# Loads held back where the attention's zone opens, and a second bank for retention's products

## The chip, the cores and the metric

The kernel runs on one core of a Trainium2 chip. The core has a matrix engine (PE, with a queue of weight loads PEld), VectorE (DVE), ScalarE (ACT), GpSimd (POOL) and a queue (SP) from which all of this kernel's transfers between the chip's memory and the core are issued. The engines run side by side and wait for each other through semaphores. The metric is the time of one execution in device microseconds (us), the median of several runs.

## The reference

One layer of a streaming encoder works on a prompt of 2048 rows and on a sample of 64 rows whose stream already has 4096 past rows. Rows are normalised and multiplied with one wide input weight; its columns feed a differential attention (four heads, queries and keys in two halves of 64, values of 128), a retention (four heads of 128, computed in chunks with a state that is carried on), a gate for each, and two merging gates. Both branches are projected, merged, projected once more and added to the input.

```python
h = rmsnorm(x, norm_g) @ w_in
qa, ka, va, za, qb, kb, vb, zb, ga, gb = jnp.split(h, _split_points(), axis=-1)
# attention: a = softmax(q0 k0) - lam * softmax(q1 k1), chunk-causal, with a distance bias
s = jnp.einsum('bqhcd,bkhcd->bhcqk', q, k) * (DK_A ** -0.5)
a = p[:, :, 0] - lam * p[:, :, 1]
# retention: inside a chunk, and across chunks by a state r
s = jnp.einsum('bnthd,bnshd->bnhts', qc, kc) * d_intra
intra = jnp.einsum('bnhts,bnshe->bnthe', s, vc)
return decay_c * r + u_n, r
cross = jnp.einsum('bnthd,bnhde,ht->bnthe', qc, r_before, xi)
...
m = ga * (oa @ w_oa) + gb * (ob @ w_ob)
return x + m @ w_out
```

Keys, values and the retention state are outputs too.

## The kernel before, in words

All products run at full precision by splitting a float32 operand into a high and a low part (names hi and lo, `thi` and `tlo`, `wh` and `wl`): three products stand for one. ACT copies the high part, DVE or POOL subtracts it for the low part.

The work has three zones. In the first the prompt's first half and the sample are projected (`w_stream`, line 2594 and after; its products are L997 and L847), and the sample's attention runs. In the second, the attention's zone, the second half is projected while the prompt's attention and the retention run among these products. In the third both branches are gated, projected and merged (L2302 to L2304, L2426 to L2428).

The order of PE, ACT and DVE is written out by a planner: the class keeps generators as tasks, each with a priority, and a clock in ns for each engine (`self.pe`, `self.act`, `self.dve`). `loop` (L160) always advances the task of best priority that is ready at PE's planned time; a generator that yields a time sleeps until PE's clock has reached it, one that yields a function sleeps until it is true. `take` and `give` hand out buffers and banks with the planned time at which they come free; `either` (L650) takes from whichever of several has one earliest. The projections have the last priority, so they fill PE when nothing else is ready. The order of SP and POOL isn't written out: the framework's scheduler places their instructions, and each of these queues runs in its order, so a transfer that waits holds up all behind it.

What matters here:

- `attn_zone` (L2672) opens the second zone. Then `z_stream` (L2685) starts three tasks: retention (`ret_stream`, L2071), the loading of heads (`h_loader`, L1468) and of query tiles (`q_loader`, L1455). `load_head` (L1415) takes two K buffers and two V buffers for each half of the keys; there are four of each, so in the first half of the prompt a second head can be loaded while the first is worked on. Four K transfers of 256 KB and two V transfers of 512 KB make up a head there; a query tile is four transfers of 128 KB, and two of them and the distance table `dfar` are loaded within the first head's loading.
- `qk_block` (L1498) makes score products (L1514, L1515) into a bank `s` or `tp`; DVE adds the distance table and takes the extremes (L1523); ACT exponentiates (L1554); `at_pv` (L1586) transposes (L1626) and multiplies with V (L1604 to L1606) into the bank `pv`.
- `fin_va` (L1232) ends a projected value tile: ACT copies the high part into the one `thi` buffer (L1245) and the raw values (L1247), DVE makes the low part (L1249), and three stores send them out (`vN<-thi`, `out_v_prompt`, `vN<-tlo`). The next tile's `thi` can't be written until the store of the last has landed. `fin_qk` uses the same `thi` buffer for keys and queries (L1216, L1211; stores `kT<-thi`, `qT<-thi`).
- `ret_block` (L1949) works on 128 rows of retention: it loads qbT, kbT and vbN, makes scores (L1970) in bank `s`, transposes keys in bank `at`, makes the output (L2004, L2007) in bank `pv`, normalises it, transposes it in bank `tp` (L2043) and stores it. `ret_some` runs eight blocks after loading two tables (rmask, rxi), two of them alive at a time. `ret_stream` runs blocks 0 to 7 once the first keys, queries and values are projected, and later the sample's block and blocks 8 to 15.

PSUM has eight banks: two `mm`, two `s`, two `at`, one `pv`, one `tp`.

Of the kernel before, what the change touches and what calls it, by code (L numbers as in the profile page):

```python
# [43 lines left out]
LAND = 2000.0  # L44
DMA_LAT = 2600.0
QUANT = 6
GRAIN = 64
EARLY = 7104
LATER = 12032
# [39 lines left out]
class Arena:  # L89
    def __init__(self, tile, n):  # L90
        self.tile = tile
        self.at = [0.0] * (n // GRAIN)
        self.turn = 0
# [10 lines left out]
    def place(self, sizes, now):  # L104
        got = []
        for n in sizes:
            k = -(-n // GRAIN)
            best = None
# [13 lines left out]
        t = max(max(w) for a, k, w in got)  # L122
        return [Span(self.tile[:, a * GRAIN:a * GRAIN + n], a, n) for (a, k, w), n in zip(got, sizes)], t

    def drop(self, span, t, lo, hi):
        a, b = span.start + lo // GRAIN, span.start + -(-hi // GRAIN)
        self.at[a:b] = [t] * (b - a)
        self.turn += 1
# [7 lines left out]
class Hybrid:  # L136
# [62 lines left out]
    def fits(self, n):  # L199
        w = -(-n // GRAIN)  # L200
        run = 0
        for t in self.ar.at:
            run = run + 1 if t is not None and t <= self.pe else 0
            if run == w:
                return True
        return False
# [1261 lines left out]
    def h_loader(self, half):  # L1468
        for h in range(4):
            yield from self.head_in(half, h)  # L1470
            yield from self.load_head(half, h)

    def chunks(self, nk):
        n = nk // 128
        if n <= 4:
            return [(0, nk)]
        if n > 8:
            m = [(0, 512), (512, 512)]
            return m + [(1024 + a, b) for a, b in self.chunks(nk - 1024)]
        last = 4 if n != 5 else 3  # L1480
        return [(0, nk - 128 * last), (nk - 128 * last, 128 * last)]
# [467 lines left out]
    def ret_block(self, k, t0, r, first):  # L1949
# [11 lines left out]
        t = self.ld(vb, self.vbN[t0:t0 + r, :], 1 << 18)  # L1961
# [7 lines left out]
        for h in range(4):  # L1969
            nc.tensor.matmul(s3[:, h, :], kt[:, h, :], qt[:, h, :], start=True, stop=True)  # L1970
            t = self.P(512)
        yield from self.take("at")
        kn = self.psum("at")[:r]
        for h in range(4):
            nc.tensor.transpose(kn[:, 128 * h:128 * h + 128], kt[:, h, :], self.ident)
            t2 = self.P(256)
# [19 lines left out]
            tu = self.P(512)  # L1996
        yield lambda: self.ret_at == k
        yield max(ts, self.t_state)
        yield from self.take("pv")
        state = self.state  # L2000
        op = self.psum("pv")[:r]
        for h in range(4):
            oh = op[:, 128 * h:128 * h + 128]
            nc.tensor.matmul(oh, sm[:, h, :], vb[:, 128 * h:128 * h + 128], start=True, stop=first)  # L2004
# [5 lines left out]
        if first:  # L2010
            nc.vector.tensor_copy(state, up)
            t = self.V(512, tu)
        else:
            for h in range(4):
# [3 lines left out]
                t = self.V(128, max(tu, to))  # L2018
# [7 lines left out]
        t1 = self.A(512, to)  # L2026
        nc.scalar.copy(o, op)
        t2 = self.A(512, to)
        self.give("pv", t2)
        yield t1  # L2030
        nc.vector.tensor_reduce(ms, sq.rearrange("p (h e) -> p h e", h=4), axis=AX.X, op=ALU.add)
        nc.vector.tensor_scalar(ms, ms, 1.0 / 128, EPS, op0=ALU.mult, op1=ALU.add)
# [1 line left out]
        t = self.V(80)  # L2034
# [2 lines left out]
        nc.vector.tensor_mul(o3, o3, rs.unsqueeze(2).to_broadcast([r, 4, 128]))  # L2037
        t = self.V(632, t2) + SLACK
        yield t
        yield from self.take("tp")  # L2040
        tp = self.psum("tp")[:, :4 * r]
        for h in range(4):
            nc.tensor.transpose(tp[:, r * h:r * h + r], o[:, 128 * h:128 * h + 128], self.ident[:r, :r])  # L2043
            t = self.P(256)
        res = qk[:, 0:4 * r]
        nc.scalar.copy(res, tp)
        t = self.A(4 * r, t)
        self.give("tp", t)
        yield t
        for h in range(4):  # L2050
            rh = res[:, r * h:r * h + r]
            d3 = self.obT[h].rearrange("p (g c) -> p g c", c=GW)
            if r == 128:
                g0, c0 = t0 // 256, t0 % 256
                t = self.st(d3[:, g0, c0:c0 + 128], rh, 1 << 16)
            else:
                t = self.st(d3[:, :, 256:GW], rh.rearrange("p (g c) -> p g c", c=8), 1 << 17)
# [12 lines left out]

    def ret_stream(self):  # L2071
        yield lambda: "kqv00" in self.done
        yield from self.ret_some(0, 8)
        yield lambda: "ret1" in self.done
        yield self.marks["ret1"] + 6000
        yield from self.ret_sample()
        yield from self.ret_some(8, 8)
        yield self.t_state
        self.st(self.o["ret_prompt"][0, 0].rearrange("h d e -> d h e"),
                self.state.rearrange("p (h e) -> p h e", h=4), 1 << 18)  # L2080
# [745 lines left out]
```

## Time and profile before

| | |
|---|---|
| median of three runs | 1929.72 us (1927.65 to 1930.25) |
| the profiled execution's own time | 1932.02 us |
| its span, first to last instruction | 1929.9 us |
| PE busy | 1887.0 us, 98% |
| DVE, ACT, POOL busy | 1291.6, 947.8, 587.9 us |
| granted clock of PE, mean | 0.993 |
| moved by DMA | 313.10 MB, 162 GB/s |

How to read it: PE is the busiest engine; a busy share of 98% is modelled from when products start and is no measure of their efficiency. What can be gained without changing the work is PE's idle time (1929.9 - 1887.0 = 42.9 us) and time at a lower clock. In the rows below `out<-in` names the tiles, L a line of the kernel before, `<-` in a row of waits the instruction that ended the wait.

### The profile page before, as it was taken

To read this page: it belongs to the slowest core of one execution; us is meant where nothing else is said; L and a number is where in the kernel's file an instruction comes from. 1 tells how busy PE (TensorE), PEld (TensorE's weight loads), DVE (VectorE), ACT (ScalarE), POOL (GpSimd) and SP (SyncE) were. 2 spreads that over 40 slices of the span, in tenths; PEclk is the share of its full clock that TensorE was granted. 3 is DMA by queue.
4 is the path that set the end of the run, shared out by engine and by line. 5 is a ranking of instruction groups with operands and counts; after the bars stand their busy time and mean duration, and the time that the engine had idled before them with its cause. 6 is when DMAs were issued, how large, how long until landed. Compare 5 with 4: busy or idle time off the path is not lost.

```text
span 1929.9 us, 33596 instructions
## 1 busy us (share of the span) xinstructions
PE 1887.0 (98%) x11690; PEld 1689.4 (88%) x11690; DVE 1291.6 (67%) x3058; ACT 947.8 (49%) x2151; POOL 587.9 (30%) x557
## 2 busy tenths in 40 slices
PE   9999999999995899999999999999999999999999
PEld 7788888888885899989999989999999999999887
DVE  6766766656573688775667675338877359987664
ACT  6444554444431566555456555346556455553221
POOL 2320365656540121121111111121211255522442
PEclk9999999999998899999999999999999999999999
DMA  7655455565658476455434444553441388886542
GB/s 253 215 167 138 160 170 178 177 181 177 181 162 222 146 194 194 148 162 143 131 91 134 135 115 113 141 142 92 112 121 52 113 233 272 249 264 197 185 153 77
DMA packets 361324, 313.10 MB, mean 162 GB/s; under 512 B 67906, under 2 KB 319938, under 8 KB 361155
## 3 DMA queue, kind: packets, MB, share of 16 engines
q1 hardware_dynamic: 361154, 310.97, 54.9%
q8 instruction: 92, 1.51, 0.3%
q14 instruction: 78, 0.63, 0.1%
HBM read 205.43 MB, written 104.60 MB: 161 GB/s over the span
## 4 chain that ended last, share of the span: by engine, by line
PE 89%; DVE 3%; DMA 3%; SPq 1%; issue 1%; ACT 1%; POOL 0%; DVEq 0%; ACTq 0%; POOLq 0%
PE mm L997 35%; PE mm L847 9%; PE tp L847 4%; PE at L1626 3%; PE s L1514 2%; PE s L1515 2%; PE s L847 2%; PE pv L1606 2%; PE pv L1605 2%; PE pv L1604 2%; PE s L2426 1%; PE s L2428 1%; PE s L2427 1%; SPq L234 1%; PE pv L1891 1%
## 5 line engine op out<-in xcount | busy, mean ns | idle before, releaser
L961 POOL TENSOR_TENSOR wl<-ws,wh 128x512 fp32r<-128x512 f32 x125 | 169.8, 1374 | 325.4 <-ACT wh L951 218.3
L997 PE MATMUL mm<-xh,wh 128*128 128x512 f32 (+2 forms) x768 | 257.7, 336 | 0.0
L997 PE MATMUL mm<-xh,wl 128*128 128x512 f32 (+2 forms) x768 | 251.5, 327 | 0.0
L997 PE MATMUL mm<-xl,wh 128*128 128x512 f32 (+2 forms) x768 | 251.4, 327 | 0.0
L997 PE MATMUL mm<-wh,xh 128*128 128x256 f32 (+1 forms) x760 | 248.0, 326 | 0.0
L997 PE MATMUL mm<-wh,xl 128*128 128x256 f32 (+1 forms) x760 | 242.4, 319 | 0.0
L997 PE MATMUL mm<-wl,xh 128*128 128x256 f32 (+1 forms) x760 | 242.2, 319 | 0.0
L1641 DVE TENSOR_TENSOR atl<-at,ath 128x512 fp32r<-128x512 f32 (+1 forms) x144 | 93.6, 659 | 100.1 <-ACT ath L1639 100.0
L1554 ACT ACTIVATE row<-row,a_mx 128x896 f32<-128x896 f32 (+5 forms) x144 | 149.5, 1041 | 21.3 <-DVE a_mx L1533 21.2
L997 PEld LDWEIGHTS mm<-wh,xh 128*128 128x128 f32 x760 | 144.7, 190 | 11.1 <-DVE raw L1169 0.2
L997 PEld LDWEIGHTS mm<-wl,xh 128*128 128x128 f32 x760 | 144.8, 191 | 10.8
L997 PEld LDWEIGHTS mm<-xh,wl 128*128 128x128 f32 x768 | 144.8, 189 | 10.6
L997 PEld LDWEIGHTS mm<-xh,wh 128*128 128x128 f32 x768 | 145.0, 189 | 10.4
L997 PEld LDWEIGHTS mm<-xl,wh 128*128 128x128 f32 x768 | 145.2, 189 | 10.0
L997 PEld LDWEIGHTS mm<-wh,xl 128*128 128x128 f32 x760 | 144.5, 190 | 10.6
L1639 ACT CAST ath<-at 128x512 fp32r<-128x512 f32 (+1 forms) x144 | 79.7, 564 | 146.1 <-PE at L1626 143.4
L1398 POOL TENSOR_TENSOR r_y<-r_y,r_sq 128x256 f32<-128x256 f32 x32 | 28.4, 888 | 388.4 <-DVE r_sq L1395 242.8
L1514 PE MATMUL s<-K,q 128*128 128x512 f32 (+3 forms) x242 | 91.7, 380 | 26.4 <-DVE a_acc L1523 25.7
L1523 DVE CUSTOM_DVE_ANT_0 row<-s,dfar 128x512 f32<-128x512 f32 (+2 forms) x144 | 88.9, 629 | 41.9 <-PE s L1515 41.8
L726 POOL TENSOR_TENSOR wl<-ws,wh 128x256 fp32r<-128x256 f32 x64 | 57.1, 892 | 195.8 <-ACT wh L717 190.8
L1576 DVE SCALAR_TENSOR_TENSOR row<-row,a_w 128x896 f32<-128x896 f32 (+6 forms) x88 | 98.3, 1125 | 0.0
L951 ACT CAST wh<-ws 128x512 fp32r<-128x512 f32 x128 | 76.9, 618 | 26.2 <-DMA ws<-in_w_in_dram 11.9
(488 smaller groups left out, 5464.8 us busy)
## 6 DMA issues: line engine op xcount, KB each, us to landing
ws<-in_w_in_dram SPq DMA_DIRECT2D x160, 256.0 KB, 3.3
q<-qT SPq DMA_DIRECT2D x128, 128.0 KB, 3.1
K<-kT SPq DMA_DIRECT2D x48, 256.0 KB, 4.3
V<-vN SPq DMA_DIRECT2D x24, 512.0 KB, 5.7
row<-in_x_prompt_dram SPq DMA_DIRECT2D x16, 512.0 KB, 4.7
wz<-in_w_in_dram SPq DMA_DIRECT2D x32, 256.0 KB, 4.1
row<-in_cache_k_T_dram SPq DMA_DIRECT2D x32, 256.0 KB, 3.7
row<-in_cache_v_diff_dram SPq DMA_DIRECT2D x32, 256.0 KB, 3.2
```

What stands on the lines that cost most here:

```text
L726: nc.gpsimd.tensor_sub(l[:, cs], src, h[:, cs].bitcast(F32))
L847: nc.tensor.matmul(ps, w[:, c], xs[x][c], start=bool(tag) and c == 0 and i == 0, stop=c == 3 and i == 2, skip_group_check=True)
L951: self.nc.scalar.copy(h, st)
L961: self.nc.gpsimd.tensor_sub(l, st, h.bitcast(F32))
L997: nc.tensor.matmul(ps, p, q, start=c == 0 and i == 0, stop=c == KC - 1 and i == 2)
L1514: nc.tensor.matmul(ps, q1s, kk, start=True, stop=False)
L1523: nc.vector.tensor_tensor_reduce(out=row[:, k0:k0 + n], in0=ps, in1=tab, scale=-SLOPES[h], scalar=3.0e38, op0=ALU.add, op1=ALU.min, accum_ ...
L1554: nc.scalar.activation(u, u, AF.Exp, bias=mx, scale=-1.0, accum_out=lp[:, k:k + 1])
L1576: nc.vector.scalar_tensor_tensor(out=u0, in0=u1, scalar=w[:, 0:1], in1=u0, op0=ALU.mult, op1=ALU.add)
L1626: nc.tensor.transpose(at[:, w:w + 128], src, self.ident)
L1639: nc.scalar.copy(ah[:, :w], at[:, :w])
L1641: nc.vector.tensor_sub(al[:, :w], at[:, :w], ah[:, :w].bitcast(F32))
```

## The change

Three things are edited. First, in `h_loader` the task sleeps for 18 us of PE's planned time after the first head of the first half has been loaded, before it loads the second. Second, `ret_stream` sleeps for 36 us of planned time before it loads the tables and starts its blocks. Third, the output products of a retention block, which took bank `pv`, and its transposes, which took bank `tp`, now each take whichever of the two is free earlier. The numbers of lines below the edits move by one to four in the changed kernel.

```diff
@@ constants
 QUANT = 6
+CALM = 18000.0
 GRAIN = 64
@@ h_loader
         for h in range(4):
             yield from self.head_in(half, h)
             yield from self.load_head(half, h)
+            if half == h == 0:
+                yield self.pe + CALM
@@ ret_block
         yield lambda: self.ret_at == k
         yield max(ts, self.t_state)
-        yield from self.take("pv")
+        bank = yield from self.either(1, "pv", "tp")
         state = self.state
-        op = self.psum("pv")[:r]
+        op = self.psum(bank)[:r]
...
         nc.scalar.copy(o, op)
         t2 = self.A(512, to)
-        self.give("pv", t2)
+        self.give(bank, t2)
...
-        yield from self.take("tp")
-        tp = self.psum("tp")[:, :4 * r]
+        bank = yield from self.either(1, "tp", "pv")
+        tp = self.psum(bank)[:, :4 * r]
...
         t = self.A(4 * r, t)
-        self.give("tp", t)
+        self.give(bank, t)
@@ ret_stream
         yield lambda: "kqv00" in self.done
+        yield self.pe + 2 * CALM
         yield from self.ret_some(0, 8)
```

## The prediction, made before the changed kernel ran

> **What bounds the kernel now.** I read the page first, then the waits of the matrix engine (PE) over the whole span, then the waits and the queue of the window in which the longest of them falls.
>
> The page's busy line, and of its forty slices (48.2 us each) the rows of PE and of the clock granted to it:
>
> ```profile
> PE 1887.0 (98%) x11690; PEld 1689.4 (88%) x11690; DVE 1291.6 (67%) x3058; ACT 947.8 (49%) x2151; POOL 587.9 (30%) x557
> PE   9999999999995899999999999999999999999999
> PEclk9999999999998899999999999999999999999999
> ```
>
> PE is busy nearly everywhere, so this kernel gets faster only where PE idles or runs at a lower clock. It idles 1929.9 - 1887.0 = 42.9 us, and one pair of slices (579 to 675 us) stands out, in the clock too. The waits of PE over the span, longest first (us in total, times, longest):
>
> ```profile
> PE s L1514 <- DVE a_acc L1523: 25.7, 1, 25.7
> PE at L2303 <- DVE ogl L2259: 3.8, 3, 1.8
> ```
>
> One single wait is 60% of all idle time. It lies at the opening of the attention's zone; of the waits in the window 596 to 633 us these two stand behind it:
>
> ```profile
> DVE tlo L1249 <- ACT raw L1247: 35.9, 2, 33.7
> ACT thi L1245 <- DMA vN<-thi: 33.3, 1, 33.3
> ```
>
> So PE's score product waits for a bank that VectorE (DVE) must read; DVE stands in its order behind the low half of a projected value tile; that waits for ScalarE (ACT), and ACT waits to overwrite the one thi buffer until the store of its last contents has landed. The DMA queue (SP) shows why that store is late (start us, us to issue):
>
> ```profile
> 594.91 0.34 SPq L234 DMA_DIRECT2D dnear<-in_c_dnear_dram  x1
> 595.30 2.40 SPq L234 DMA_DIRECT2D K<-kT  x4
> 597.75 5.68 SPq L234 DMA_DIRECT2D q<-qT  x8
> 603.48 0.59 SPq L234 DMA_DIRECT2D dfar<-in_c_dfar_dram  x1
> 604.11 1.06 SPq L234 DMA_DIRECT2D V<-vN  x2
> 605.21 6.05 SPq L234 DMA_DIRECT2D K<-kT  x4
> 611.31 1.91 SPq L234 DMA_DIRECT2D V<-vN  x2
> 613.27 6.54 SPq L234 DMA_DIRECT2D row<-in_c_rmask_dram  x1
> ...
> 623.38 1.58 SPq L234 DMA_DIRECT2D row<-vbN  x1
> 625.06 0.38 SPq L239 DMA_DIRECT2D vN<-thi  x1
> ```
>
> The store leaves at 625.06 behind 30 loads. The last 14 of them are head 1's K and V (heads counted from 0), from 605.21, and retention's tables and first two blocks, to 625.06: 19.9 us of the queue. The chain that ended last runs through it (start us, us):
>
> ```profile
> 611.94 11.42 DMA V<-vN
> ...
> 625.06 5.17 DMA vN<-thi
> ...
> 632.39 0.58 PE s L1514
> ```
>
> The store lands at 630.23, and 2.16 us later PE runs again.
>
> **Part 1: the 14 loads are held back (h_loader, ret_stream).** The planner's two new waits put head 1's loads 18 us, retention's 36 us of planned PE time later. In the built program the queue is the same up to the second V load; then come at once the three stores of the waiting tile, then one K load, the next tile's stores and the q loads. The number of instructions is the same on all engines (PE 11390, DVE 3060, ACT 1924, POOL 562, SP 1415 as built), so only waits can change. PE's order too is the same for its first 2,614 rows, beyond the stall, so the stall's place stays.
>
> The store can issue from 605.2. When does it land? Landings of the thi stores and of head 0's two V loads, in their windows:
>
> ```profile
> L239 SPq DMA_DIRECT2D vN<-thi x3: 360/368/379, 590.9 to 630.9; - x3
> DMA to landing us min/median/max: 2.2/2.5/5.2
> L234 SPq DMA_DIRECT2D V<-vN x2: 432/506/581, 604.1 to 604.6; - x2
> DMA to landing us min/median/max: 6.2/8.8/11.4
> ```
>
> What the 16 DMA engines moved from 594 to 606 us, and from 605 to 627:
>
> ```profile
> DMA packets 1698, 2.45 MB, mean 204 GB/s; under 512 B 208, under 2 KB 1313, under 8 KB 1698
> DMA packets 7487, 5.88 MB, mean 267 GB/s; under 512 B 293, under 2 KB 6643, under 8 KB 7486
> ```
>
> - Early end: the store does not feel the loads ahead and lands in 2.2 us, at 607.4; PE resumes at 609.6; gain 632.4 - 609.6 = 22.8 us.
> - Late end: it lands behind the second V load, which landed at 604.59 + 11.4 = 616.0; its 0.26 MB at 267 GB/s take 1.0 us; landed 617.0, PE at 619.1; gain 13.3 us.
> - My value: up to that V load 3.9 MB were issued (dnear 256, four K of 256, eight q of 128, dfar 480, two V of 512 KB). At most 2.45 MB had moved by 606; the other 1.45 MB at 267 GB/s last to 611.4, the store's own data to 612.4, and the 2.5 us of a lone store less its 1.0 us of data are 1.5 us to the landing: 613.9, PE at 616.1. I take this, nearer the late end, because that V load landed late with head 1's K loads beside it. Gain **16.3 us**.
>
> The clock. Windows around the stall (from:to, length, then busy time and count of PE, PEld, DVE, ACT, POOL; granted clock; DMA share; GB/s):
>
> ```profile
> 609.00:610.00 1.00, 0.00 (x0) 0.00 (x0) 0.00 (x0) 0.00 (x0) 0.00 (x0) 1.00 1.27 301
> 610.00:611.00 1.00, 0.00 (x0) 0.00 (x0) 0.00 (x0) 0.00 (x0) 0.00 (x0) 0.58 1.15 284
> 632.00:637.00 5.00, 4.61 (x16) 4.32 (x17) 3.32 (x17) 3.62 (x13) 2.55 (x2) 0.50 0.77 236
> 637.00:638.00 1.00, 1.00 (x8) 0.90 (x7) 0.71 (x3) 0.70 (x3) 0.83 (x1) 0.76 0.88 257
> ```
>
> PE stopped at 632.39 - 25.72 = 606.7 and the clock halved at about 610.2, 3.5 us later; after the restart it stayed at half for about 5 us, which costs 2.5 us. A stall of 616.1 - 606.7 = 9.4 us still halves it: no gain here, cost unchanged. Only at the early end (2.9 us idle) do 2.5 us come on top.
>
> The Trainium skill (TensorE: Matmul & The Clock Gate, Part 1) has the clock halve after an idle window of about 3.4 us that runs freely, and full again after about 3.4 us of work. The 3.5 us agree, the 5 us are longer here. By its figure the restart would cost some 1.7 us instead of 2.5, before and after alike, so an estimate by that page leaves the sum as it is.
>
> **What the held loads cost where they go.** Built order: three K and two V loads follow the fourth tile's stores, head 1's q loads follow, then eight retention loads, then a K load of head 2 that needs PE's last score product of head 0, and behind that the store of the first key tile's thi. PE's rate here:
>
> ```profile
> 640.00:890.00 250.00, 244.81 (x1979) 239.38 (x1978) 197.79 (x580) 146.11 (x360) 45.55 (x39) 1.00 0.58 167
> ```
>
> That is 7.9 products a us. Head 1's first score product is PE row 2858, some 240 rows past the stall's end, 30 us: even with the slowest landing quoted, 11.4 us, its K are in time if the queue reaches them within 18 us. The key store waits for row 2839, 52 rows (6.6 us) after its transposes; with 2.5 to 5.2 us to land, the buffer is free 9.1 to 11.8 us after them, and ACT wants it after row 2861, 74 rows or 9.4 us. So 0 to 2.4 us; I take **1 us** lost, inside these ends.
>
> **Part 2: retention's products and transposes take bank pv or tp.** Nothing is added. With the delay it moves the first half's blocks 2 to 7, which ran behind head 3 (PE rows 4587 to 4941), among heads 1 to 3 (all eight products in rows 3068 to 4234). Attention's last PE row goes from 7871 to 7503 while the last projection stays (8151, 8149): filler is used later, in all the same work. DVE instructions of a block:
>
> ```profile
> L1979 DVE TENSOR_TENSOR row<-s,row x17: 417/691/693, 654.8 to 1255.8; 128x512 f32<-128x512 f32 x16, 64x256 f32<-64x256 f32 x1
> L2016 DVE SCALAR_TENSOR_TENSOR row<-row,at x64: 273/284/290, 680.6 to 1263.0; 128x128 f32<-128x128 f32 x64
> L2031 DVE TENSOR_REDUCE ms<-row x17: 671/685/686, 671.5 to 1263.6; 128x4 f32<-128x512 f32 x16, 64x4 f32<-64x512 f32 x1
> L2037 DVE TENSOR_TENSOR row<-row,sm_y x17: 683/691/694, 682.8 to 1267.3; 128x512 f32<-128x512 f32 x16, 64x512 f32<-64x512 f32 x1
> ```
>
> 0.69 + 4 x 0.28 + 0.69 + 0.69 = 3.2 us a block, 19 us for six, into a window in which DVE has 250 - 198 = 52 us free. I take 0: PE's filler covers it while DVE has room. If that cover goes, all 19 us at worst; the other way, the window's own idle of 5.2 us could go, a gain of 5.2. In the last part the earlier end of attention lets output weights be split sooner; of PE's waits there (3.8 us on L2259) I count none as gone, 0 to 3.8.
>
> **Sum.** -16.3 + 1 + 0 = -15.3 us. The profiled execution took 1932.0 us (span 1929.9 and 2.1 around it), 2.3 above the median 1929.7; I carry the difference to the median: **1914.4, say 1915 us**.
>
> **Rivals.**
> - The store lands unhindered (early end): -22.8 - 2.5 + 1 = -24.3, 1905 us. For it speaks the 2.2 us; against it, that in this window transfers landed in the order of issue (V at 6.2, then 11.4 us). The Trainium skill (DMA: Bandwidth & Descriptors, on queues, rings and completion order) says that each DMA engine takes its descriptors in the ring's order; by that rule this rival falls and the sum stays at 16. No run here has yet shown a store with few loads ahead.
> - Slower: the held loads block the queue where they now stand, ahead of the key tiles' stores. Price: the same 19.9 us of queue, whole, and a second halving of the clock of 2.5: -16.3 + 19.9 + 2.5 = +6.1, 1936 us. It decides once the hold is beyond 14 us. For it: ACT again has one thi buffer, and 14 loads and a PE-bound K load stand ahead. Against: they go in two bunches and the window's DMA share is 0.58.
> - DVE becomes the bound among heads 1 to 3: half of the 19 us shows in PE: -15.3 + 9.6 = -5.7, 1924 us. For it: 0.79 of DVE busy there becomes 0.87. Against: PE lost only 5.2 us at 0.79.
> - The hold-back does not shorten the wait, because something else was late too (dnear, q or K): 1930 us. Against: of the loads ahead, the eight q were the last that the scores need, and they landed by 602.9 + 5.6 = 608.5:
>
> ```profile
> L234 SPq DMA_DIRECT2D q<-qT x8: 573/605/606, 597.7 to 602.9; - x8
> DMA to landing us min/median/max: 4.4/5.3/5.6
> ```
>
> **How the numbers follow.** Forecast 0.54, unhindered store 0.11, DVE bound 0.16, queue blocked 0.13, no effect 0.06. A measurement here tells 0.2%, 3.9 us, from no change. Faster: 0.54 + 0.11 + most of 0.16 = 0.78; same: 0.06 and the edge of the DVE case, 0.09; slower 0.13. The likeliest case alone spans 1911 to 1920 (13.3 with 2.4 lost, to 16.3 with 2.4 of the last part's 3.8 gained). The range reaches to the unhindered store and the lost effect, 1905 to 1930, and leaves out the blocked queue and the tail of the DVE case.
>
> **What would show it.** The wait of PE on L1523 near 606 us falls from 25.7 to 8 to 12 us (3 if the store is unhindered), ACT's on vN<-thi from 33.3 to about 17; the clock still halves once. SP issues vN<-thi right behind two V loads near 605 to 608. The first retention product comes after 670 us. The prediction is wrong if a new wait of ACT on kT<-thi or of PE over 10 us appears between 620 and 950 us, or if PE's idle time there passes 10 us.

## The result and the profile after

The changed kernel takes 1904.2 us (median of four runs, 1903.6 to 1906.9), the kernel before on the same chip 1929.2: a ratio of 0.9874 with a 95% interval of 0.9857 to 0.9891. It is faster by 25 us where 15 were forecast, and 0.8 us below the low end of the range. The profiled execution took 1906.88 us with a span of 1904.8, 25.1 less than the span before, so the two traces can be set against each other as they stand.

The page's busy line of the changed kernel, and of its forty slices the rows of PE and of its granted clock:

```profile
PE 1886.2 (99%) x11690; PEld 1691.2 (89%) x11690; DVE 1277.7 (67%) x3058; ACT 947.4 (50%) x2151; POOL 590.5 (31%) x557
PE   9999999999998999999999999999999999999999
PEclk9999999999998999999999999999999999999999
```

PE's busy time is the same within 0.8 us; its idle time went from 42.9 to 18.6 us. Its waits over the whole span, longest first (us in total, times, longest), and then the waits of the window 596 to 633 us:

```profile
PE s L1517 <- DVE a_acc L1526: 8.1, 2, 7.9
PE at L2307 <- DVE ogl L2263: 3.1, 3, 2.0
```

```profile
DVE tlo L1250 <- ACT raw L1248: 18.8, 3, 15.8
ACT thi L1246 <- DMA vN<-thi: 15.4, 1, 15.4
PE s L1517 <- DVE a_acc L1526: 7.9, 1, 7.9
```

The stall is at its old place with its old chain, and shorter: 7.9 us for 25.7, behind a wait of ACT on the store of 15.4 us for 33.3. The DMA queue (SP; start us, us to issue) shows the store right behind head 0's V loads, as the built order had it; the only held load that follows closely is one K load:

```profile
597.53 6.02 SPq L235 DMA_DIRECT2D q<-qT  x8
603.60 0.60 SPq L235 DMA_DIRECT2D dfar<-in_c_dfar_dram  x1
604.24 1.06 SPq L235 DMA_DIRECT2D V<-vN  x2
605.39 2.43 SPq L240 DMA_DIRECT2D vN<-thi  x1
...
608.99 0.71 SPq L235 DMA_DIRECT2D K<-kT  x1
612.87 0.35 SPq L240 DMA_DIRECT2D vN<-thi  x1
```

Those V loads, and the copy of ACT that waited for the store (the bracket is ACT's idle time and what ended it):

```profile
L235 SPq DMA_DIRECT2D V<-vN x2: 432/506/581, 604.2 to 604.7; - x2
DMA to landing us min/median/max: 5.6/6.2/6.7
```

```profile
612.26 0.59 ACT L1246 CAST thi<-mm 128x512 fp32r<-128x512 f32 x1 [15.41 <-DMA vN<-thi]
```

The slower V load took 6.7 us instead of 11.4, so it had landed by 604.7 + 6.7 = 611.4, and ACT could write thi at 612.26, where the prediction had the store landing at 613.9. A store issued at 605.39 took until 612.26, 6.9 us, though stores elsewhere land in 2.2.

The rest of the gain lies elsewhere. Windows of the changed kernel (from:to, length, then busy time and count of PE, PEld, DVE, ACT, POOL; granted clock; DMA share; GB/s), and after them the second one in the kernel before:

```profile
640.00:890.00 250.00, 249.55 (x2050) 245.68 (x2050) 197.26 (x581) 150.48 (x378) 50.27 (x42) 1.00 0.63 180
1510.00:1700.00 190.00, 186.95 (x1445) 183.43 (x1444) 134.46 (x267) 89.81 (x195) 74.84 (x65) 0.99 0.72 213
```

```profile
1510.00:1700.00 190.00, 185.53 (x1415) 180.59 (x1414) 140.25 (x256) 104.11 (x219) 95.91 (x79) 1.00 0.78 233
```

In 640 to 890 us PE idled 250 - 244.81 = 5.2 us before and idles 0.45 now; around the opening of the last zone it idled 4.5 and idles 3.05. Retention moved into the first of these windows, as one of its DVE instructions, run once per block, shows before and after (busy us, mean ns, idle us before):

```profile
L2031 DVE TENSOR_REDUCE ms<-row 128x4 f32<-128x512 f32 x2 | 1.4, 677 | 0.0
```

```profile
L2034 DVE TENSOR_REDUCE ms<-row 128x4 f32<-128x512 f32 x8 | 5.4, 678 | 0.0
```

So the 25.1 us of span are: the stall 17.8, the window behind it 4.8, the opening of the last zone 1.4, and 1.1 in small pieces (PE's busy time 0.8 of it). Of the signs that the prediction named, PE's wait came just under its 8 to 12 us, ACT's was 15.4 for about 17, retention's first output product came at 687.7 us, after 670, and no wait of ACT on kT<-thi appeared from 620 to 950 us. The clock halved once at the stall, and in this profile a second time at 1578 us.

### The profile page after: what moved, and what is told of

Read it like the earlier page. It is cut to its first block, busy times and chain, and to the rows that moved or that the text cites. A ratio compares the mean times of both kernels' runs of the same rounds, so it can differ in the third digit from the quotient of the medians.

```text
span 1904.8 us, 33589 instructions
## 1 busy us (share of the span) xinstructions
PE 1886.2 (99%) x11690; PEld 1691.2 (89%) x11690; DVE 1277.7 (67%) x3058; ACT 947.4 (50%) x2151; POOL 590.5 (31%) x557
## 5 line engine op out<-in xcount | busy, mean ns | idle before, releaser
L998 PEld LDWEIGHTS mm<-wl,xh 128*128 128x128 f32 x760 | 144.5, 190 | 10.9
L1526 DVE CUSTOM_DVE_ANT_0 row<-s,dfar 128x512 f32<-128x512 f32 (+2 forms) x147 | 90.5, 631 | 26.0 <-PE s L1518 25.4
L1307 ACT COPY ev<-mm 128x512 f32<-128x512 f32 (+2 forms) x84 | 38.6, 460 | 113.2 <-PE mm L998 105.1
```

The costliest lines, as they stand in the source:

```text
L998: nc.tensor.matmul(ps, p, q, start=c == 0 and i == 0, stop=c == KC - 1 and i == 2)
L1526: nc.vector.tensor_tensor_reduce(out=row[:, k0:k0 + n], in0=ps, in1=tab, scale=-SLOPES[h], scalar=3.0e38, op0=ALU.add, op1=ALU.min, accum_ ...
```

## The experiments

My theory was that the change is the shorter stall and nothing else: the held loads make it, the bank choice is worth 0, and all else is hidden. The rivals: that the bank choice brings part of the gain (or takes part back), that one hold alone does it, and that something besides the loads ahead of the store sets when it lands. Head 1's hold-back alone wasn't tried, nor the products' choice of bank without a hold.

A table first, worked out from the profiles: PE's idle time in us in the stall, in 640 to 890 us and in 1510 to 1700 us (length of the window less PE's busy time), the start of retention's first output product, and by how many us the attention's last V product lies ahead of the last projection product.

| kernel | median us | stall | 640-890 | 1510-1700 | retention from | attention ahead |
|---|---|---|---|---|---|---|
| before | 1929.2 / 1927.3 | 25.7 | 5.2 | 4.5 | 667 | 49 |
| after | 1904.2 | 7.9 | 0.45 | 3.05 | 688 | 110 |
| holds without bank choice | 1923.8 | 8.4 | 0.06 | 13.2 | 901 | 33 |
| transposes' bank choice alone | 1925.2 | 22.8 | 3.45 | 2.7 | 664 | 62 |
| retention's hold alone | 1915.8 | 16.8 | 2.35 | 0.5 | 685 | 83 |
| retention's hold, bank choice | 1912.2 | 17.1 | 1.2 | 0.5 | 681 | 109 |
| after, first V loads later | 1900.4 | 6.3 | 0.0 | 0.7 | 686 | 110 |
| both holds, retention's short, no choice | 1906.5 | 8.1 | 4.1 | 1.0 | 657 | 59 |
| after, hold of 19 us | 1903.2 | 8.0 | 1.05 | 1.1 | 687 | 110 |
| before with a second thi buffer | 1912.1 | 15.7 | 0.13 | 2.0 | 657 | 53 |

(1929.2 is the kernel before beside the first run of the changed kernel, 1927.3 beside the others but the last two of this section.)

**Both holds, the bank choice undone.**

```diff
-        bank = yield from self.either(1, "pv", "tp")
+        yield from self.take("pv")
...
-        bank = yield from self.either(1, "tp", "pv")
+        yield from self.take("tp")
```

> Both hold-backs, without the choice of bank (pv and tp as before). The opening of the zone is the changed kernel's, so the wait of PE near 606 us is 7.9 us by every theory. Theory 'bank' (the choice of bank gives the 6 us gained outside that wait): PE idles some 5 us in 640 to 890 us as before, and the time is about 1910 us. Theory 'hold' (the loads and retention standing later gives them): PE idles under 1 us there, 1904 us. Theory 'order' (any new order of the planner falls somewhere within some us): either, without rule.

Measured: 1923.84 us, ratio 0.9982 (0.9972 to 0.9991). None of the theories had this time: the window from 640 to 890 us idles 0.06 us, the sign of 'hold', but 1904 us didn't come with it. The stall is nearly as short as in the changed kernel, and yet 20 us of the 25 are gone again. Where they went, in its windows, its waits of PE from 1540 to 1600 us, and its first retention products (count, ns min/median/max, first and last start), followed by those of the changed kernel:

```profile
640.00:890.00 250.00, 249.94 (x1989) 244.11 (x1989) 179.77 (x526) 145.79 (x350) 48.34 (x43) 1.00 0.57 167
...
1510.00:1700.00 190.00, 176.83 (x1344) 172.50 (x1343) 151.01 (x272) 101.20 (x212) 92.88 (x77) 0.97 0.77 236
```

```profile
PE s L2310 <- DVE w_o_retl L2116: 3.5, 1, 3.5
PE s L2308 <- ACT w_o_reth L2109: 2.9, 1, 2.9
PE s L2309 <- DVE ogl L2265: 2.7, 2, 1.5
```

```profile
L2008 PE MATMUL pv<-row x136: 269/275/320, 901.4 to 1249.6; 128*128 128x128 f32 x128, 64*64 64x128 f32 x8
```

```profile
L2007 PE MATMUL tp<-row x104: 270/275/275, 687.7 to 1248.2; 128*128 128x128 f32 x104
L2007 PE MATMUL pv<-row x32: 269/275/321, 1099.7 to 1231.6; 128*128 128x128 f32 x24, 64*64 64x128 f32 x8
```

Held back and confined to the bank pv, retention's output starts at 901 us, not at 688 in tp: 213 us later. Of its first eight blocks none has its output products before 890 us here, in the changed kernel all eight (0 and 64 of these products). The attention is done only 33 us before the projections instead of 110, and at the opening of the last zone PE waits for output weights and for gated rows (`ogl`) that ACT and DVE split too late: 13.2 us idle for 3.05, and a mean clock of 0.97 there. Against the changed kernel the profiled span is 14.9 us longer: 10.0 of it idle time (10.9 more in 1550 to 1600 us, 0.9 less elsewhere) and 4.9 busy time, of which the lower clock in 1550 to 1600 us (0.90 for 0.97, some 7 us more at half clock) can be 3.5. The other 5 us between the medians lie in the difference of the profiled executions from their medians (2.2 below here, 2.7 above for the changed kernel) and aren't located. So beside both holds the bank choice is worth 20 us, and my 0 for it was wrong in kind: with it the delayed retention runs early. It takes both holds to bring this about; with retention's alone, below, pv is found at 685 us.

**The transposes' bank choice alone.** Neither hold; the products take pv as before, and the transposes may take tp or pv.

```diff
-        yield self.pe + 2 * CALM
...
-        bank = yield from self.either(1, "pv", "tp")
+        yield from self.take("pv")
+        bank = "pv"
```

(The first line stands for both holds; the transposes keep `either`.)

> No hold-back; only retention's transposes choose between tp and pv, its products stay on pv. The queue's order at the opening is that of before, so PE waits 25.7 us near 606 us by every theory. Theory 'bank': 1923 to 1926 us. Theory 'hold': 1929 us, PE's idle time in 640 to 890 us about 5 us. Theory 'order': within some 5 us of 1929 either way.

Measured: 1925.15 us, ratio 0.9989 (0.9979 to 0.9998). PE's longest wait is

```profile
PE s L1515 <- DVE a_acc L1524: 24.4, 3, 22.8
```

still 22.8 us in one piece, where 25.7 was expected: the same loads stand ahead of the store, but they were issued faster, and it left at 621.90 instead of 625.06. Half of the bank choice without holds brings some 2 us. The time suits 'bank' and 'order' alike, so this run doesn't tell them apart; what the products' choice does without holds isn't known.

**Retention's hold alone,** and **retention's hold with the bank choice.** Of the changed kernel the first takes out head 1's hold and the bank choice, the second head 1's hold only.

```diff
-            if half == h == 0:
-                yield self.pe + CALM
```

> Retention alone is held back; head 1's four K and two V loads (2.1 MB) stand ahead of the store again. If the store's place in the stream of bytes sets the wait: it lands 2.1 MB / 267 GB/s = 7.9 us later than in the changed kernel, 620.2 us, and PE waits 15.7 us near 606 us, about 10 less than before. Rival (the two hold-backs work only together, because the last loads ahead decide): the wait stays above 22 us. Whole time 1919 us if nothing else is won, 1913 us if 'hold' is right and retention's place gives the rest.

> As the run before, with the choice of bank for products and transposes. PE's wait near 606 us is 15.7 us again. Theory 'bank': some 6 us faster than the run with retention's hold-back alone, 1913 us. Theory 'hold': equal to it within 1 us. Theory 'order': a difference of some us of either sign.

Measured: 1915.78 us, ratio 0.9946 (0.9928 to 0.9964), and 1912.21 us, ratio 0.9916 (0.9901 to 0.9931). PE's longest wait in the first and in the second:

```profile
PE s L1515 <- DVE a_acc L1524: 17.0, 2, 16.8
```

```profile
PE s L1515 <- DVE a_acc L1524: 18.3, 2, 17.1
```

Each hold takes its part of the stall: 25.7 to 16.8 or 17.1 with the eight retention loads gone, and to 7.9 with head 1's six gone as well. The store's issue moved as the prediction's count of the queue says (19.9 us for all fourteen loads): from 625.06 to 611.25 us with retention's gone and to 605.39 with head 1's gone too. The wait moved otherwise, 8.6 to 8.9 and then 9.2 us, since the store itself takes longer behind the loads: from the start of its issue to ACT's copy 5.3, 9.8 and 6.9 us. The 7.9 us that the expectation worked out from 2.1 MB were 8.8 (621.04 for 612.26), and the rival that one hold alone does nothing fell. The bank choice is worth some 3.6 us beside retention's hold alone, between the 6 of 'bank' and the 1 of 'hold', with intervals that overlap. Both have some 4 us less idle at the opening of the last zone than before; there the attention is done 83 and 109 us ahead.

**The first head's V loads later.** The changed kernel, with the two V loads of head 0 held back by 6 us of planned time, so that the store goes ahead of them.

```diff
+        if half == h == 0:
+            yield self.pe + 6000.0
         for u in range(nu):
```

> The changed kernel, and head 0's own two V loads (1.05 MB) held back 6 us of planned time too; in the built queue the stores of the waiting tile then stand right behind dfar. If bytes ahead of the store set the wait (267 GB/s, measured in the kernel before), it lands 3.9 us earlier, at 608.4 instead of 612.35 us, PE waits 4.0 us instead of 7.9, and the time is about 1900 us. Rival: the V loads come too late for the first products with V, and a wait of at least 4 us appears there: 1904 us or more.

Measured: 1900.44 us, ratio 0.9859 (0.9838 to 0.988). Its DMA queue and the copy that waited:

```profile
603.22 0.59 SPq L235 DMA_DIRECT2D dfar<-in_c_dfar_dram  x1
603.91 0.38 SPq L240 DMA_DIRECT2D vN<-thi  x1
...
605.47 1.98 SPq L235 DMA_DIRECT2D V<-vN  x2
```

```profile
610.84 0.59 ACT L1246 CAST thi<-mm 128x512 fp32r<-128x512 f32 x1 [13.85 <-DMA vN<-thi]
```

With the V loads behind it the store still takes 610.84 - 603.91 = 6.9 us, with dnear, K, q and dfar ahead. That speaks against an unhindered landing in 2.2 us as long as these loads are under way. The expectation by bytes had the landing at 608.4 and a wait of 4.0 us, and 610.84 and 6.3 came: here the copy starts 1.4 us sooner than in the changed kernel's first profile, as the store is issued 1.5 us sooner. The time is as expected all the same, and the rival's wait on the V loads didn't appear. The repeat below gives a larger step.

**Both holds, retention's only 10 us, no bank choice.**

```diff
-        yield self.pe + 2 * CALM
+        yield self.pe + 10000.0
```

(and the bank choice undone, as above)

> Both hold-backs without the choice of bank, as in the run of the hold-backs alone, but retention sleeps 10 us of planned time instead of 36. The opening's wait should be 8 us again. Theory 'late attention' (without the choice of bank, retention's products find pv free only after head 3, so attention ends too near the end of the projections, and PE runs dry at the start of the output zone): the first blocks get in early, attention ends some 45 us before the projections instead of 33, PE's idle time from 1540 to 1700 us falls from 13 to 3 to 6 us, 1908 to 1914 us. Rival (that idle time is the planner's accident in this one order): no relation to the distance of the two ends.

Measured: 1906.48 us, ratio 0.989 (0.9872 to 0.9907). Retention now begins at 657 us in pv, the attention ends 59 us ahead, and the last zone's opening idles 1.0 us. So the 20 us of the first experiment come with holding retention that long beside head 1 with pv alone, and either the bank choice or a shorter hold avoids them. How the shorter hold does it isn't shown: only one of the eight blocks has its output products before 890 us (two in the kernel before, none in the first experiment), and why that moves the attention's end by 26 us is open. So the rival, an accident of that one order, isn't excluded: over the table the idle time at the last zone doesn't follow the distance strictly (4.5 us at 49, 1.0 at 59, 2.7 at 62, 3.05 and 0.7 at 110), and only the 13.2 at 33 stands apart. The window behind the stall, however, idles nearly as before in this kernel:

```profile
640.00:890.00 250.00, 245.87 (x1946) 239.48 (x1945) 186.43 (x543) 142.32 (x342) 50.84 (x42) 1.00 0.57 168
```

**The changed kernel with a hold of 19 us** (38 for retention), to see whether the length matters in itself.

```diff
-CALM = 18000.0
+CALM = 19000.0
```

> The changed kernel with 19 and 38 us instead of 18 and 36: the planner makes another order, for no reason of the hardware. It shows how much the order alone moves. The opening's wait stays 7.9 us. If the 6 us gained outside it belong to the change, the time is within 2 us of 1904; if they are an accident of one order, 1904 to 1911 us.

Measured: 1903.24 us, ratio 0.9873 (0.9856 to 0.989), a stall of 8.0 us: the same kernel in effect.

**The kernel before with a second thi buffer** for value tiles in the attention's zone, its memory taken from the zone's row buffers.

```diff
-LATER = 12032
+LATER = 11520
...
-            yield from self.take("thi")
+            high = yield from self.either(1, "thi", "thx")
```

> The kernel before, in which value tiles of the attention's zone may use a second buffer for their high part (the room is taken from the arena of score rows, 512 of 12032 columns). The loads stand ahead of the stores as before. If the one thi buffer behind a late store is what stops PE, PE runs on past 606 us until the next value tile, some 6 us of products later, and waits there until the store has landed near 630 us: the wait falls from 25.7 to some 19 us and begins 6 us later. Rival (PE would have waited for something else at 606 us anyway): a wait of over 24 us begins at 606 us again.

Measured: 1912.14 us, ratio 0.9919 (0.9893 to 0.9946; two runs). The fourteen loads stand where they stood and the stores leave at 623.92; PE's wait is now another one, 8.8 us later, and the window behind it no longer idles (some 19 us of wait and 6 us later were expected; the rival, a wait for something else at 606 us, fell):

```profile
PE mm L997 <- DVE tlo L1254: 15.7, 1, 15.7
```

```profile
640.00:890.00 250.00, 249.87 (x2017) 244.79 (x2016) 191.66 (x563) 148.85 (x365) 50.65 (x44) 1.00 0.57 168
```

The one buffer and the late store are two halves of one cause: another buffer lets PE work on until 615.5 us and takes 10 us of the stall, the holds take 17.8.

**The changed kernel and the later V loads side by side** on one chip, both unaltered from above.

> The changed kernel itself, beside the next one on one chip. Both readings (the later V loads gain, or the two are the same and the earlier 1900.4 against 1904.2 us came from the chips) expect 1902 to 1906 us here, a ratio to before of 0.987 to 0.989. It also tells whether the 2.0 us wait in the output part, with the halved clock behind it, comes in every execution: if so the median is near the profiled 1906.9, if not it is nearer 1903.

> First head's V loads 6 us of planned time later, on the same chip as the changed kernel. If the store's place before the V loads is worth something: 1.5 us less wait, one clock window less at half speed at times (1.7 us), so 2 to 4 us below the kernel of the run beside it, outside its spread. If not: within 1 us of it.

Measured: 1903.53 us (1903.18 to 1908.27; ratio 0.9876, 0.9861 to 0.989) and 1900.22 us (1898.68 to 1901.18; ratio 0.9854, 0.9838 to 0.9871). The times don't overlap: holding the V loads too is worth 3.3 us and gives the fastest version here. ACT's copy in the first and in the second:

```profile
612.71 0.59 ACT L1246 CAST thi<-mm 128x512 fp32r<-128x512 f32 x1 [16.01 <-DMA vN<-thi]
```

```profile
609.31 0.59 ACT L1246 CAST thi<-mm 128x512 fp32r<-128x512 f32 x1 [12.92 <-DMA vN<-thi]
```

It starts 3.4 us sooner: the store is issued 1.7 us sooner (603.35 for 605.00) and takes 6.0 us to the copy instead of 7.7. PE's wait is 5.4 us for 8.5. Over all profiles the store takes 6.9 to 7.7 us with the V loads right ahead of it (five kernels) and 6.9 and 6.0 with them behind, so their bytes do cost something, and that the first two profiles both show 6.9 is chance. In the profiled execution of the changed kernel (1908.27 us) the 2.0 us wait in the last zone came again, without a halved clock behind it, and PE idled 1.6 us in 640 to 890 us, where the first profile had 0.45. Its other three executions lie at 1903.2 to 1903.6; whether they have that wait isn't shown.

## Why the prediction was right and where it was wrong

- **The stall: mechanism right, size a little off.** Place, chain, order of the queue and the loads named were as forecast, and the runs with one hold show the wait taken off piece by piece. The gain was 17.8 us where 16.3 were put. The number that was off is the landing, taken near the late end because of the second V load's 11.4 us. In the five kernels that have head 1's K loads right behind that V load it took 7.8 to 11.4 us, in the five that don't 6.7 to 7.4: part of the 11.4 was due to these loads, which the change removes, and part was that execution's. With 6.7 us the store was through by 612.26. That the sum came so near is partly luck: it counts bytes at one rate, and the runs follow that only roughly (8.8 us for 7.9, 1.4 and 3.4 for 3.9).
- **The unhindered store fell,** as argued: 6.9 to 7.7 us with the V loads ahead, 6.0 and 6.9 with them behind, not 2.2. The Trainium skill (DMA: Bandwidth & Descriptors, on queues, rings and completion order) has each DMA engine take its descriptors in the ring's order; the trace is in line with it, with the V loads landed by 611.4 and the store behind them by 612.26, though landings alone can't show in which order descriptors were taken.
- **The clock: no gain and no cost, right.** After the restart it stayed at half for 4.8 us in the changed kernel, 5.1 before. Why it was "longer here" than 3.4 is told below; the reason wasn't known then.
- **The loss of 1 us where the held loads go: not there.** No wait of ACT on kT<-thi (one of 1.1 us on qT<-thi) and no wait of PE above 0.5 us shows between 640 and 890 us in the first profile. 0 was inside the ends given.
- **Part 2, taken as 0: the step that failed.** The window's own 5.2 us had been named as the end on the gain side and were then not counted, on the ground that PE's other work covers what moves; 4.8 of them came (3.6 in the second profile). They don't need the bank choice, under which they had been put: with both holds and without it the window idles 0.06 us. DVE, which the rival feared, is busy 197.26 us there after 197.79. Retention's own DVE lines rose there, with eight blocks for two, from 7.4 to 25.4 us, 18 for the 19 that were forecast to move in, and as much other work went out. The window is nearly free of idle time in two kernels that begin retention late (0.06 with a start at 901 us, 0.45 at 688) and in the one with a second buffer (0.13 at 657); it idles 1.05 to 2.35 in three that begin at 681 to 687, and 4.1 with both holds and a start at 657, so the start alone doesn't set it. Before, 3.0 of the 5.2 us were score products waiting for q loads, at 766, 767 and 843 us, over 130 us behind the stall. Which alteration puts these in time was not told apart, so the cause of this gain stays open, and the second profile of the changed kernel leaves 1.6.
- **The last zone, taken as 0 of 0 to 3.8:** 1.4 us came. That the end of the attention matters there fits the one far case: with 33 us PE runs dry for 13.2 us. Beyond that the table shows no strict rule.
- **What the prediction didn't see** is that the parts hang together. It added three edits up, and priced the bank choice by what it moves in DVE. The first experiment shows that the holds without it are worth 3.5 us and with it 25.
- **The range** had its low end from the unhindered store alone. By its own ends, 5.2 of part 2 and 3.8 of the last zone on top of the likeliest 15.3 reach 24.3 us too, without that rival; and the stall's early end lay beyond. These bounds had to be joined to the forecast before the range was closed. The 10.2 us between 1914.4 and 1904.2 are 4.8 + 1.4 here, 1.5 in the stall, 1.0 not lost, and 1.1 in small pieces, but for 0.4 of rounding and of the profiles against their medians.

The slower rivals didn't come: the held loads didn't block the queue ahead of the key tiles' stores (no wait of ACT on kT<-thi and no wait of PE above 0.5 us from 620 to 950 us), and DVE didn't become the bound.

## What to carry to other kernels

A store that frees a lone buffer belongs ahead of loads which nobody needs yet: look for it in the DMA queue by the wait that it ends, and count the loads before it. When a hold delays a second task, look up which banks and buffers are free at its new time; here the same delay was worth 25 us with a second bank and 3.5 without, and with a shorter delay of the second task 21 without. And when an end of a bound is a named stretch of idle time in the very window that a change re-orders, put part of it into the sum and all of it into the range.

## What the runs showed of the hardware that was not expected

**The clock follows windows of 3.41 us that don't start with the work.** In all twelve profiles the stretch at half clock around the stall is a whole number of them (2, 3, 5, 6, 7 or 8 times 3.41 us, from the moments where the mean clock of a one-microsecond window lies between 0.5 and 1). The changed kernel cut at its own borders:

```profile
605.47:608.88 3.41, 0.99 (x9) 0.78 (x7) 0.00 (x0) 0.00 (x0) 0.00 (x0) 1.00 1.11 317
608.88:612.29 3.41, 0.00 (x0) 0.00 (x0) 0.00 (x0) 0.03 (x1) 0.00 (x0) 0.50 1.15 335
612.29:615.71 3.42, 1.39 (x6) 1.39 (x7) 1.89 (x9) 2.97 (x9) 1.61 (x2) 0.50 0.88 298
615.71:619.12 3.41, 3.41 (x12) 3.09 (x11) 2.18 (x9) 2.40 (x8) 0.98 (x2) 0.50 0.60 168
619.12:622.53 3.41, 3.41 (x30) 3.37 (x29) 2.36 (x12) 2.92 (x9) 1.27 (x1) 1.00 0.69 205
1574.86:1578.27 3.41, 1.43 (x12) 1.22 (x11) 3.38 (x5) 2.55 (x6) 2.92 (x4) 1.00 0.73 212
1578.27:1581.68 3.41, 3.41 (x18) 3.41 (x18) 3.41 (x7) 2.17 (x6) 2.42 (x3) 0.50 0.88 270
```

and the kernel with the second thi buffer:

```profile
613.43:616.85 3.42, 2.06 (x18) 1.85 (x16) 0.00 (x0) 0.00 (x0) 0.00 (x0) 1.00 1.08 199
616.85:620.26 3.41, 0.00 (x0) 0.00 (x0) 0.00 (x0) 0.00 (x0) 0.00 (x0) 1.00 1.17 295
...
630.50:633.91 3.41, 2.70 (x12) 2.50 (x13) 3.31 (x12) 2.16 (x6) 0.00 (x0) 0.50 0.90 259
633.91:637.33 3.42, 3.42 (x18) 3.42 (x18) 1.82 (x4) 0.00 (x0) 0.00 (x0) 0.50 1.02 228
```

The clock halves behind a window in which PE was busy 0.99 of 3.41 us (29%), and even behind one with 1.43 (42%), a wait of 2.0 us; it doesn't behind one with 2.06 (60%). It comes back behind a full window, not behind one with 2.70 (79%). So the halving comes 2.4 us (here) to 4.8 us (there) after the last product, as the window's phase falls, and a restart runs at half clock for 3.3 us where it meets a border (the later V loads) and for 6.1 us where PE begins a little after one (the second buffer), half of which is lost. The Trainium skill (TensorE: Matmul & The Clock Gate, Part 1) states a freely running window of 3413 ns, and these traces agree with it; how much of a window must be idle or busy is read from the rows here. It also means that 2 us of wait may cost 1.7 more or nothing: in the profile shown at 1578 us it did, in the second profile of the same kernel it didn't.

**A store's issue is held up too.** A store of thi that takes 0.35 us of the queue at 612.87 took 2.43 us to issue right behind the V loads (2.4 to 3.1 in the five kernels that have it there), 5.4 in the two that have head 1's six loads ahead as well, and 0.38 when ahead of the V loads. The load of rmask, 6.54 us in the kernel before, took 0.56 in the run with the short hold. In the seven held-up cases ACT's copy starts 4.4 to 4.6 us after the end of the issue, so the longer wait is in the issue. What holds it up isn't shown.
